# A two-layer streaming-encoder trunk on one core: two groups share their first halves of K at the start, and one more chunk is done in seven products at the end

## The chip, the cores and the metric

The kernel runs on one core of one Trainium2 chip. The metric is the device time of one execution in microseconds (us), as a median over runs. The engines are TensorE (PE in the profile, with its weight loads as PEld), VectorE (DVE), ScalarE (ACT), GpSimd (POOL) and SyncE (SP). SP and ACT issue the DMAs here, on a queue each; the rows of those issues stand under SPq and ACTq.

## The reference, cut to what matters

Two layers (DEPTH = 2) of 256 frames with 1024 channels in float32:

```python
for i in range(2):
    x = x + 0.5 * swiglu(rmsnorm(x, ffn1_norm[i]), w_gate, w_up, w_down)   # d_ff = 2816
    proj = rmsnorm(x, mix_norm[i]) @ w_in[i]
    ...                                       # self-attention (chunked, or differential), memory attention
    x = x + concat([o_s, o_m]) @ w_out[i]
    x = x + 0.5 * swiglu(rmsnorm(x, ffn2_norm[i]), w_gate, w_up, w_down)

def swiglu(h, w_gate, w_up, w_down):
    return (silu(h @ w_gate) * (h @ w_up)) @ w_down
```

The change touches the first half-step of layer 0 (its start) and the second half-step of layer 1 (the last work of the kernel).

## The kernel before, in words

**Products.** Every float32 operand is split into a high part `hi` (a cast to the type fp32r, by ACT at L338) and a remainder `lo` = operand - `hi` (by DVE at L356). A product of a 128x128 block of x with a 128x512 block of weights is three matmuls of 512 columns in `dense`: hi by xh (L511), lo by xh (L514), hi by xl (L517). So each block of weights costs one cast and one remainder before PE can use it, and PE does them all in the order in which they were recorded.

**Weights.** They come in chunks of four blocks into three buffers `raw` (`NRAW = 3`), all loads issued by SP (L294). In `ffn`, a gate-and-up chunk (g, c) holds 256 columns of `w_gate` and 256 of `w_up` of group g (of NG = 11), for the half c of K = 1024: four blocks k of 128 rows. Group g adds up in two PSUM banks `gu`, one for each half-tile of 128 frames (tb = 0, 1), over both chunks, (g, 0) and then (g, 1). The first chunk of the kernel is loaded in eight pieces of 128 KB (gate and up of each block), the second in four of 256 KB, later ones in two of 512 KB.

**x.** It stands in two tiles, `x0` and `x1` (x_85 and x_86 in the order), one for each tb. `prep_half(xt, tb, hf, ...)` takes one half hf of 512 channels: four transposes on PE (`xtp`, L525), y = transposed x by the gain (DVE, L557), xh (ACT cast, L560), xl (DVE, L562). Channel half hf is K half c of the first products. The squares of x for the norm are summed by ACT (`junk`, L574) and come in later, as a factor of the result. Four sums and differences of the y tiles (L780) with casts and remainders `xf` (L784, L787) follow for a pair of groups that is done with seven products.

**The start.** `start_gain` and `start` are threads with times written by hand. In between PE does some products of the identity (`warm`). The load of ACT's function table is asked for by `table_hint`.

**Down.** The down chunks c = 0 to 10 (256 rows of `w_down` each) take 8 products of 3 matmuls. A chunk in the table `SEVEN` takes 7: `seven_item` forms four sums of weight blocks (`wsum`, DVE), and `seven_forms` four sums of the hidden values (`sf`); results go to four more banks `m`, which `seven_sums` adds into x after the last such chunk. The first such chunk holds two pairs of hi and lo buffers; a later one (`guest`) puts part of its blocks into the room of xh and xl (`gxh`, `gxl`), of which there is one.

**What sets the order.** The program is recorded by threads in a small planner (`Flow`) with a clock of its own, estimated durations (`flow.act`, `flow.dve`) and arrival times for loads (`dma_free`, `LAT`); each engine then does its instructions in the recorded order. The last small loads (`late_loads`, among them the rows `grow` of gains) are issued by SP one behind each later chunk; PE transposes `grow` (`gps`, L231) 8 us of the planner's clock after the last.

**DMAs and semaphores.** Each DMA gets one of eight completion semaphores (DMAHW0 to DMAHW7 in the order below), one after the other in the order of the built program, whichever queue issues it. A DMA that gets a semaphore which an earlier one has used waits, where it is issued, for that one's landing.

Of the kernel before, what the change touches and what calls it, by code (L numbers as in the profile page):

```python
# [16 lines left out]
AF = mybir.ActivationFunctionType  # L17
# [3 lines left out]
P = 128  # L21
# [121 lines left out]
def kernel(  # L143
# [10 lines left out]
    nc = tc.nc  # L154
    PSUM = bass.MemoryType.PSUM
    NRAW, NHL, NT2 = 3, 4, 19
    flow = Flow()
# [19 lines left out]
    def bank(name, shape=(P, 4, P)):  # L177
        return banks.take(list(shape), F32, name)
# [3 lines left out]
    nc.scalar.dma_start(out=g1row, in_=ffn1_norm.rearrange("l (k p) -> (l k) p", p=P))  # L182
    xs = [const.tile([P, D], F32, name=f"x{tb}") for tb in range(2)]

    def load_x(tb, hf, queue=None):
        (queue or nc.sync).dma_start(out=xs[tb][:, hf * 512:(hf + 1) * 512],
                                     in_=x[0, tb * P:(tb + 1) * P, hf * 512:(hf + 1) * 512])

    load_x(0, 0)
    load_x(1, 0, nc.scalar)  # L190

    ident = const.tile([P, P], F32, name="ident")
    make_identity(nc, ident)
# [78 lines left out]
    raw_left = [NRAW]  # L272
    hl_left = [NHL]
    xt_room = [False]
    dma_free = [2.5]
    LAT = 1.5
    at = [0]

# [4 lines left out]
    def add_chunk(parts, uses=8, w=1):  # L283
        return Item([add_raw(parts)], uses, w)

    def loader():
        for i, c in enumerate(chunks):
            yield lambda: raw_left[0] > 0
            raw_left[0] -= 1
            c.raw = wraw.tile([P, 2048], F32, tag="raw", name=f"raw{i}")  # L290
            dma_free[0] = max(dma_free[0], flow.now)
            n = len(c.parts)
            for j, (dst, src) in enumerate(c.parts):
                nc.sync.dma_start(out=dst(c.raw), in_=src)  # L294
                dma_free[0] += 2.9 / n
                if i < 2 and j % 2:
                    for q in range((j - 1) * 4 // n, (j + 1) * 4 // n):
                        c.block[q] = dma_free[0] + LAT
                if i == 1 and j == 1:
                    load_x(1, 1)  # L300
                    dma_free[0] += 0.7
            c.arrive = dma_free[0] + LAT
            c.block = [t or c.arrive for t in c.block]
            if i == 0:
                load_x(0, 1)
                dma_free[0] += 0.7
            if i > 4 and late_done[0] < len(late_loads):
                dst, src = late_loads[late_done[0]]
                late_done[0] += 1
                nc.sync.dma_start(out=dst, in_=src)  # L310
                dma_free[0] += 0.3
# [56 lines left out]
    def cols4(w, c, c0, n, o, pieces=1):  # L368
        st = 4 // pieces
        return [((lambda raw, a=a: k4(raw)[:, a:a + st, o:o + n]),  # L370
                 w[c * 512 + a * P:c * 512 + (a + st) * P, c0:c0 + n].rearrange("(k p) n -> p k n", p=P))
                for a in range(0, 4, st)]
# [1 line left out]
    def rows2(w, r):  # L374
        return [(lambda raw: k2(raw), w[r * 256:(r + 1) * 256, :].rearrange("(k p) n -> p k n", p=P))]

    SEVEN = {(0, 1): (), (0, 2): (1, 4, 7), (1, 1): (1, 4, 7), (1, 2): (1, 4, 7)}
    PAIR = {(0, 1): 4, (0, 2): 3, (1, 1): 3, (1, 2): 3}

    def turned2(w, r):  # L380
        src = w[r * 256:(r + 1) * 256, :].rearrange("(k b i) n -> b i k n", k=2, b=4)
        return [((lambda raw, b=b: k2(raw)[b::4]), src[b]) for b in range(4)]
# [6 lines left out]
    def seven_item(it, guest):  # L389

        r = [it.own(q) for q in range(4)]
        t = lambda j: lambda: it.t[j]
        it.n, it.uses, it.takes, it.gives, it.guest = 1 if guest else 2, 7, 4, 4, guest
        it.sums = [(r[1], r[0]), (r[3], t(0)), (r[3], r[1]), (r[2], t(1))]
        it.units = [(r[0], 0, 1, None), (r[2], 1, 1, None), (r[3], 2, 1, None)] + [(t(j), 3 + j, 1, j) for j in range(4)]
# [46 lines left out]
    def plan_ffn(l, nm, wg, wu, wd):  # L442
        def parts(g, c):
            pieces = (4, 2)[len(chunks)] if len(chunks) < 2 else 1
            a = cols4(wg[l], c, g * 256, 256, 0, pieces)
            b = cols4(wu[l], c, g * 256, 256, 256, pieces)
            return [q for ab in zip(a, b) for q in ab]

        gu = {}
        pair = PAIR[l, nm]  # L450
        work = [(g, c) for g in range(NG) for c in range(2)]
        if pair is not None:
            rest = [w for w in work if w[0] not in (pair, pair + 1)]
            n = 2 * pair
            p = iter(rest[n:])
            work = rest[:n]
            loads = {}
            for x in ("11", "m1", "p", "12", "m5", "p", "22", "m7", "p", "m6", "p", "m3", "p", "p", "21", "m2", "p", "m4"):
                work.append(next(p) if x == "p" else x)
            work += list(p)  # L460
            blocks = {"11": (pair, 0), "12": (pair + 1, 0), "22": (pair + 1, 1), "21": (pair, 1)}
            raws = [Chunk(parts(*blocks[x])) for x in ("11", "12", "22", "21")]
            made, mk = pair_items(raws)
            which = dict(zip(("11", "12", "22", "21"), raws))
        for w in work:
            if w in ("11", "12", "22", "21"):
                chunks.append(which[w])
            elif isinstance(w, str):
                mk[w]()
            else:  # L470
                gu[w] = add_chunk(parts(*w), 8, 2)
        plan[l, nm, "gu"] = gu
        plan[l, nm, "work"] = [w for w in work if w not in ("11", "12", "22", "21")]
        if pair is not None:
            plan[l, nm, "pair"] = made
        dn = []
        for c in range(NG):
            dn.append(add_chunk(turned2(wd[l], c)))
            if c in SEVEN[l, nm]:
                seven_item(dn[-1], c != SEVEN[l, nm][0])  # L480
            elif c >= NG - 3:
                u = dn[-1].units
                u[1], u[2] = u[2], u[1]
        plan[l, nm, "dn"] = dn
# [133 lines left out]
    def ffn(l, nm, xt, gc_next):  # L618
        hts = [None] * NG
        htt = [None] * NG  # L620
        sv = SEVEN[l, nm]
        prog = [-1]
# [127 lines left out]
        def plain_chunk(g, c, tbs, ks=range(4)):  # L750
            if g not in open_:
                flow.until(banks.has(2))
                open_[g] = [bank(f"gu{tb}", (P, 512)) for tb in range(2)], [None, None]
                flow.spawn(evac(g, *open_[g]))
            ps, end = open_[g]
            for tb in tbs:
                for k in ks:
                    kk = 4 * c + k
                    t = dense(ps[tb], xt.h[tb][:, kk, :], xt.l[tb][:, kk, :], lambda: xt.t[tb][kk],
                              plan[l, nm, "gu"][g, c], k, kk == 0, kk == KT - 1)  # L760
                if c == 1 and 3 in ks:
                    end[tb] = t
# [85 lines left out]
        work = list(plan[l, nm, "work"])  # L848
        if (l, nm) != (0, 1):
            for tb in range(2):  # L850
                for c in range(2):
                    plain_chunk(0, c, (tb,))
        else:
            for c in range(2):
                for ks in ((0, 1), (2, 3)):
                    plain_chunk(0, c, range(2), ks)
        work = work[2:]
        for w in work:
            if isinstance(w, str):
                product(w)  # L860
# [47 lines left out]
    def table_hint(func):  # L908
        nc.scalar.activation(dummy, dummy, func)
        flow.act(1, 1.3)  # L910
# [710 lines left out]


    flow.spawn(loader(), idle=True)
    flow.spawn(split_hi(), idle=True)
    flow.spawn(split_lo(), idle=True)
# [3 lines left out]
    def start_gain():  # L1629
        tp = bank("gps0")  # L1630
        nc.tensor.transpose(out=tp[:, 0, :16], in_=g1row, identity=ident[:16, :16])
        yield flow.pe(T_TR)
        nc.vector.tensor_copy(gcol[:, 0:16], tp[:, 0, :16])
        banks.give()
        flow.dve(16)
        warm(2)
        yield 4.6
        warm(5)

    def start(tb, hf, t):  # L1640
        yield t
        yield from prep_half(xt, tb, hf, GC_FFN1, 3.0)

    def warm(n):
        for _ in range(n):
            nc.tensor.matmul(out=wb[:, 0, :], lhsT=ident, rhs=ident, start=True, stop=True)
# [1 line left out]
    wb = bank("warm")  # L1648
    banks.give()
    warm(4)  # L1650
    table_hint(AF.Silu)
    flow.now = 2.7
    flow.spawn(start_gain())
    for tb in range(2):
        for hf in range(2):
            flow.spawn(start(tb, hf, (3.4, 8.8, 5.6, 10.8)[2 * tb + hf]))
    flow.spawn(gain_columns())
    flow.spawn(rope_setup(), idle=True)
    flow.spawn(lambda_setup())
# [2 lines left out]
    for l in range(DEPTH):  # L1662
        xt = ffn(l, 1, xt, GC_MIX + l * KT)
        xt = mixer(l, xt, GC_FFN2 + l * KT)
        xt = ffn(l, 2, xt, None if l == DEPTH - 1 else GC_FFN1 + (l + 1) * KT)
# [53 lines left out]
```

## Time and profile before

| what | value |
|---|---|
| median of 3 runs | 954.87 us (954.74 to 955.77) |
| profiled execution | 955.69 us |
| its span (first to last instruction) | 953.9 us, so 1.8 us lie around it |
| granted TensorE clock | 1.0 |
| busy: PE, PEld, DVE, ACT, POOL | 945.6, 774.1, 820.0, 587.0, 109.1 us |
| HBM read and written | 188.99 MB, 14.16 MB: 213 GB/s over the span |

A busy share is an average over stages. Where PE has work without a gap, only its own work counts; where it waits, the row of the wait names what came last. In the rows of the timeline stand start, duration, engine, line, operation, tiles and, in brackets, how long the engine was idle and for what. In the rows by stretch stand length and busy time of each engine with the number of instructions, then granted clock, share of the DMA engines and GB/s. In the rows of the DMA view the last number is the median time from issue to landing.

### The profile page before, as it was taken

The numbers are of one execution on the slowest core, as the hardware profiler recorded it, in microseconds if no ns is written. First come the engines' busy times: TensorE is split into PE (matmuls) and PEld (weight loads), VectorE is DVE, ScalarE is ACT, GpSimd is POOL, SyncE is SP. The second block draws the span as 40 slices with busy tenths as digits, with TensorE's granted clock in tenths as the row PEclk, the third lists the DMA queues.
The fourth block names the chain that finished last, engine by engine and source line by source line (L and its number), as shares of the span: only waits on it lengthen the run. The fifth ranks groups of instructions, "written<-read, shape, count | busy, mean of one in ns | idle before, by whom it ended". The sixth has DMA issues, their size and how long they took to land.

```text
span 953.9 us, 13334 instructions
## 1 busy us (share of the span) xinstructions
PE 945.6 (99%) x4475; PEld 774.1 (81%) x4475; DVE 820.0 (86%) x1483; ACT 587.0 (62%) x1121; POOL 109.1 (11%) x160
## 2 busy tenths in 40 slices
PE   9999999999999999999999999999999999999998
PEld 7888888887777888888888888888787778888886
DVE  7898978888777899979889899796999888999884
ACT  6556566677676746647546656564676865665650
POOL 1000057621210100000000000000434200000000
PEclk9999999999999999999999999999999999999999
DMA  8987799486525387887746679775641367588751
GB/s 265 289 263 236 224 354 296 158 276 210 177 90 177 97 266 225 262 287 219 245 146 219 208 226 288 247 253 166 196 158 57 121 214 228 183 275 276 239 197 45
DMA packets 169887, 204.04 MB, mean 214 GB/s; under 512 B 10137, under 2 KB 145114, under 8 KB 169818
## 3 DMA queue, kind: packets, MB, share of 16 engines
q1 hardware_dynamic: 169498, 202.78, 66.0%
q8 instruction: 35, 0.57, 0.3%
q10 hardware_dynamic: 320, 0.40, 0.1%
q14 instruction: 34, 0.28, 0.1%
HBM read 188.99 MB, written 14.16 MB: 213 GB/s over the span
## 4 chain that ended last, share of the span: by engine, by line
PE 90%; DVE 6%; DMA 2%; ACT 1%; issue 1%; SPq 0%; ACTq 0%; DVEq 0%
PE gu L517 13%; PE gu L514 13%; PE gu L511 13%; PE acc L511 9%; PE acc L517 9%; PE acc L514 9%; PE pair_m L511 3%; PE pair_m L514 3%; PE pair_m L517 3%; PE pj L517 2%; PE pj L511 2%; PE pj L514 2%; DVE lo L356 2%; PE S L1360 1%; DMA x<-in_x_dram 1%; PE AV L1441 1%
## 5 line engine op out<-in xcount | busy, mean ns | idle before, releaser
L338 ACT CAST hi<-raw 128x512 fp32r<-128x512 f32 (+1 forms) x467 | 336.3, 770 | 172.6 <-DMA raw<-in_ffn_w_up_dram 45.6
L356 DVE TENSOR_TENSOR lo<-raw,hi 128x512 fp32r<-128x512 f32 (+1 forms) x467 | 391.9, 875 | 35.5 <-ACT hi L338 35.4
L514 PE MATMUL gu<-lo,xh 128*128 128x512 f32 x576 | 224.7, 390 | 0.5 <-DVE lo L356 0.5
L517 PE MATMUL gu<-hi,xl 128*128 128x512 f32 x576 | 224.5, 390 | 0.4 <-DVE xl L562 0.4
L511 PE MATMUL gu<-hi,xh 128*128 128x512 f32 x576 | 224.4, 390 | 0.0
L517 PEld LDWEIGHTS gu<-hi,xl 128*128 128x128 f32 x576 | 108.1, 188 | 23.9 <-DVE xl L562 1.7
L514 PEld LDWEIGHTS gu<-lo,xh 128*128 128x128 f32 x576 | 108.1, 188 | 23.5 <-DVE lo L356 1.4
L511 PEld LDWEIGHTS gu<-hi,xh 128*128 128x128 f32 x576 | 108.2, 188 | 22.3
L517 PE MATMUL acc<-hi,ht 128*128 128x512 f32 x280 | 109.5, 391 | 0.0
L511 PE MATMUL acc<-hi,ht 128*128 128x512 f32 x280 | 109.2, 390 | 0.0
L514 PE MATMUL acc<-lo,ht 128*128 128x512 f32 x280 | 109.1, 390 | 0.0
L338 ACT CAST hi<-wsum 128x512 fp32r<-128x512 f32 x82 | 47.7, 619 | 26.5 <-DVE wsum L350 26.5
L514 PE MATMUL pj<-lo,xh 128*128 128x512 f32 x160 | 64.0, 400 | 0.0
L517 PE MATMUL pj<-hi,xl 128*128 128x512 f32 x160 | 63.8, 399 | 0.0
L511 PE MATMUL pj<-hi,xh 128*128 128x512 f32 x160 | 63.8, 399 | 0.0
L514 PEld LDWEIGHTS acc<-lo,ht 128*128 128x128 f32 x280 | 52.6, 188 | 10.9
L517 PEld LDWEIGHTS acc<-hi,ht 128*128 128x128 f32 x280 | 52.6, 188 | 10.8
L511 PEld LDWEIGHTS acc<-hi,ht 128*128 128x128 f32 x280 | 52.6, 188 | 10.7
L532 POOL TENSOR_TENSOR xr<-v,nhalf 128x1 f32<-128x1 f32 x12 | 10.3, 861 | 435.1 <-DVE v L530 435.1
L356 DVE TENSOR_TENSOR lo<-wsum,hi 128x512 fp32r<-128x512 f32 x82 | 52.8, 680 | 0.0
L633 ACT ACTIVATE sil<-gu,xr 128x256 f32<-128x256 f32 x72 | 33.7, 468 | 29.8 <-PE gu L517 29.7
L532 POOL TENSOR_TENSOR hf<-v,nhalf 128x8 f32<-128x8 f32 (+1 forms) x20 | 31.4, 1570 | 87.3 <-DVE v L530 78.9
(232 smaller groups left out, 1429.5 us busy)
## 6 DMA issues: line engine op xcount, KB each, us to landing
raw<-in_ffn_w_down_dram SPq DMA_DIRECT2D x176, 256.0 KB, 4.5
raw<-in_ffn_w_gate_dram SPq DMA_DIRECT2D x82, 512.0 KB, 4.0
raw<-in_ffn_w_up_dram SPq DMA_DIRECT2D x82, 512.0 KB, 5.4
raw<-in_w_in_dram SPq DMA_DIRECT2D x32, 512.0 KB, 4.4
hd<-hb SPq DMA_DIRECT2D x44, 256.0 KB, 4.6
hr<-hd SPq DMA_DIRECT2D x44, 256.0 KB, 4.6
raw<-in_w_out_dram SPq DMA_DIRECT2D x8, 1024.0 KB, 5.1
raw<-in_w_mem_kv_dram SPq DMA_DIRECT2D x4, 1024.0 KB, 5.3
```

What stands on the lines that cost most here:

```text
L338: nc.scalar.copy(out=it.part(0, q, w), in_=src())
L356: nc.vector.tensor_sub(it.part(1, q, w), src(), it.part(0, q, w).bitcast(F32))
L511: nc.tensor.matmul(out=ps, lhsT=xh, rhs=wh, start=start, stop=False)
L514: nc.tensor.matmul(out=ps, lhsT=xh, rhs=wl, start=False, stop=False)
L517: nc.tensor.matmul(out=ps, lhsT=xl, rhs=wh, start=False, stop=stop)
L532: nc.gpsimd.tensor_tensor(out=dst, in0=v[:, :n], in1=nhalf[:, :n], op=ALU.pow)
L633: nc.scalar.activation(sil, ps[tb][:, 0:256], AF.Silu, scale=xt.r[tb])
L1360: nc.tensor.matmul(out=ss[e][:, pr, :nk], lhsT=q[rows, pr, :], rhs=k[rows, pr, :], start=i == 0, stop=i == len(passes) - 1)
L1441: nc.tensor.matmul(out=av[64 * e:64 * e + 64, pr, :], lhsT=vsrc(kb, pr, e), rhs=pts[e][:, pr, kb, :], start=(kb == 0), stop=(kb == nb - 1))
```

## The change

At the start: x's first half-tile is loaded in two quarters, one on each queue; x1's first half goes behind the first weight pieces on SP; both second halves go behind both first chunks. Three pieces of the first chunk move to ACT's queue (the up piece of block 0, gate and up of block 3). The table load stands behind ACT's first issues. The plan of chunks becomes (0, 0), (1, 0), (0, 1), (1, 1), and so on: groups 0 and 1 both take their first halves of K before either takes its second. The planner's arrival times and the hand-written times change with it, and there are 4 warm products for 7 ahead of the first weights. At the end: chunks 1, 3, 5, 7 of the last down phase are in `SEVEN` instead of 1, 4, 7.

```diff
-    def load_x(tb, hf, queue=None):
-        (queue or nc.sync).dma_start(out=xs[tb][:, hf * 512:(hf + 1) * 512],
-                                     in_=x[0, tb * P:(tb + 1) * P, hf * 512:(hf + 1) * 512])
-
-    load_x(0, 0)
-    load_x(1, 0, nc.scalar)
+    def load_x(tb, hf, q=0, n=2, queue=None):
+        sl = slice(hf * 512 + q * 256, hf * 512 + (q + n) * 256)
+        (queue or nc.sync).dma_start(out=xs[tb][:, sl], in_=x[0, tb * P:(tb + 1) * P, sl])
+
+    load_x(0, 0, 0, 1)
+    load_x(0, 0, 1, 1, nc.scalar)
...
-    dma_free = [2.5]
+    dma_free = [2.95]
...
             n = len(c.parts)
+            lat = LAT if i > 1 else 0.6
             for j, (dst, src) in enumerate(c.parts):
-                nc.sync.dma_start(out=dst(c.raw), in_=src)
-                dma_free[0] += 2.9 / n
+                (nc.scalar if i == 0 and j in (1, 6, 7) else nc.sync).dma_start(out=dst(c.raw), in_=src)
+                dma_free[0] += 3.0 / n
                 if i < 2 and j % 2:
                     for q in range((j - 1) * 4 // n, (j + 1) * 4 // n):
-                        c.block[q] = dma_free[0] + LAT
-                if i == 1 and j == 1:
-                    load_x(1, 1)
-                    dma_free[0] += 0.7
-            c.arrive = dma_free[0] + LAT
+                        c.block[q] = dma_free[0] + lat
+                if i == 0 and j == 1:
+                    table_hint(AF.Silu)
+                    load_x(1, 0)
+                    dma_free[0] += 0.75
+            c.arrive = dma_free[0] + lat
             c.block = [t or c.arrive for t in c.block]
-            if i == 0:
-                load_x(0, 1)
-                dma_free[0] += 0.7
+            if i == 1:
+                for tb in range(2):
+                    load_x(tb, 1)
+                    dma_free[0] += 0.75
...
-    SEVEN = {(0, 1): (), (0, 2): (1, 4, 7), (1, 1): (1, 4, 7), (1, 2): (1, 4, 7)}
+    SEVEN = {(0, 1): (), (0, 2): (1, 4, 7), (1, 1): (1, 4, 7), (1, 2): (1, 3, 5, 7)}
...
         work = [(g, c) for g in range(NG) for c in range(2)]
+        if (l, nm) == (0, 1):
+            work[:4] = [(g, c) for c in range(2) for g in range(2)]
...
+            work = work[2:]
         else:
-            for c in range(2):
-                for ks in ((0, 1), (2, 3)):
-                    plain_chunk(0, c, range(2), ks)
-        work = work[2:]
+            for ks in ((0, 1), (2, 3)):
+                plain_chunk(0, 0, range(2), ks)
+            work = work[1:]
...
-        warm(2)
-        yield 4.6
-        warm(5)
+        yield 5.2
+        warm(4)
...
-    table_hint(AF.Silu)
...
-            flow.spawn(start(tb, hf, (3.4, 8.8, 5.6, 10.8)[2 * tb + hf]))
+            flow.spawn(start(tb, hf, (3.4, 12.0, 4.6, 13.0)[2 * tb + hf]))
```

What this makes of the order. In the rows, raw_111 is the first chunk; the second is raw_121 before and raw_122 now; hi_0 with a number is a chunk's cast, and xh_130 before is xh_132 now (tb = 0), xh_131 is xh_133 (tb = 1). In brackets stand the semaphores that an instruction waits for.

ACT's first instructions before:

```order
L182 DMA g1row<-in_ffn_norm_dram 16x128
L186 DMA x_86<-in_x_dram 128x512
L909 ACT_TABLE_LOAD
L909 ACTIVATE dummy<-dummy 128x1 [waits Pool_49]
L338 CAST hi_0_168<-raw_111 128x512 [waits DMAHW4_49,DMAHW3_49]
L560 CAST xh_130<-y 128x512 [waits DVE_49]
```

and now:

```order
L182 DMA g1row<-in_ffn_norm_dram 16x128
L187 DMA x_85<-in_x_dram 128x256
L295 DMA raw_111<-in_ffn_w_up_dram 128x256
L914 ACT_TABLE_LOAD
L914 ACTIVATE dummy<-dummy 128x1 [waits Pool_49]
L295 DMA raw_111<-in_ffn_w_gate_dram 128x256 [waits DMAHW1_49]
L295 DMA raw_111<-in_ffn_w_up_dram 128x256 [waits DMAHW2_49]
L341 CAST hi_0_162<-raw_111 128x512 [waits DMAHW4_49,DMAHW3_49]
L565 CAST xh_132<-y 128x512 [waits DVE_49]
```

Two issues with a semaphore to wait for stand ahead of ACT's first cast, where none stood. Which landings they are is told by SP's issues from the sixth on, each of which waits for the semaphore that it then takes:

```order
L295 DMA raw_111<-in_ffn_w_gate_dram 128x256 [waits DMAHW0_49]
L295 DMA raw_111<-in_ffn_w_up_dram 128x256 [waits DMAHW1_49]
L295 DMA raw_122<-in_ffn_w_gate_dram 128x2x256 [waits DMAHW2_49]
L295 DMA raw_122<-in_ffn_w_up_dram 128x2x256 [waits DMAHW3_49]
L295 DMA raw_122<-in_ffn_w_gate_dram 128x2x256 [waits DMAHW4_49]
L295 DMA raw_122<-in_ffn_w_up_dram 128x2x256 [waits DMAHW5_49]
L187 DMA x_85<-in_x_dram 128x512 [waits DMAHW6_49]
L187 DMA x_86<-in_x_dram 128x512 [waits DMAHW7_49]
L295 DMA raw_129<-in_ffn_w_gate_dram 128x4x256 [waits DMAHW0_49]
L295 DMA raw_129<-in_ffn_w_up_dram 128x4x256 [waits DMAHW3_49]
```

Between the last two, numbers 1 and 2 are missing: ACT's two issues have them, for their third use. Their second use is the up piece of block 2 (raw_111, number 1) and the second chunk's first gate piece (raw_122, number 2), so these landings are what ACT's issues wait for.

DVE's order in the opening before, from its first op on raw:

```order
L356 TENSOR_TENSOR lo_0_169<-raw_111,hi_0_168 128x512 [waits DMAHW4_49,DMAHW3_49,Activation_49]
L562 TENSOR_TENSOR xl_132<-y,xh_130 128x512 [waits Activation_49]
L557 TENSOR_TENSOR y<-xtp,gcol 128x512 [waits PE_49]
L356 TENSOR_TENSOR lo_0_169<-raw_111,hi_0_168 128x512 [waits DMAHW6_49,DMAHW5_49,Activation_49]
L356 TENSOR_TENSOR lo_0_169<-raw_111,hi_0_168 128x512 [waits DMAHW7_49,DMAHW0_49,Activation_49]
L356 TENSOR_TENSOR lo_0_169<-raw_111,hi_0_168 128x512 [waits DMAHW2_49,DMAHW1_49,Activation_49]
L562 TENSOR_TENSOR xl_133<-y,xh_131 128x512 [waits Activation_49]
L557 TENSOR_TENSOR y<-xtp,gcol 128x512 [waits PE_49]
```

and now, its first two ops on raw and then the stretch up to the third chunk (raw_129, the second half of K of group 0):

```order
L359 TENSOR_TENSOR lo_0_163<-raw_111,hi_0_162 128x512 [waits DMAHW4_49,DMAHW3_49,Activation_49]
L562 TENSOR_TENSOR y<-xtp,gcol 128x512 [waits PE_49]
L567 TENSOR_TENSOR xl_134<-y,xh_132 128x512 [waits Activation_49]
L359 TENSOR_TENSOR lo_0_163<-raw_111,hi_0_162 128x512 [waits DMAHW7_49,DMAHW6_49,Activation_49]
...
L359 TENSOR_TENSOR lo_0_200<-raw_122,hi_0_199 128x512 [waits Activation_49]
L562 TENSOR_TENSOR y<-xtp,gcol 128x512 [waits PE_49] x2
L567 TENSOR_TENSOR xl_134<-y,xh_132 128x512 [waits Activation_49]
L567 TENSOR_TENSOR xl_135<-y,xh_133 128x512 [waits Activation_49]
L785 TENSOR_TENSOR y<-y 128x512 [waits DVE_49] x4
L792 TENSOR_TENSOR xf<-y,xf 128x512 [waits Activation_49]
L359 TENSOR_TENSOR lo_0_261<-raw_129,hi_0_260 128x1024 [waits DMAHW3_49,DMAHW0_49]
```

The y of tb = 1 moved ahead of the first xl, and the second halves' y and xl moved behind all eight remainders of the first two chunks; the third chunk's first remainder now has four of the sums and one xf ahead of it. On PE, whose order follows the table of chunks, the first 24 matmuls take raw_111 for both tb, the next 24 raw_122, and the transposes of x's second halves stand behind the 23rd and the 26th.

## The prediction

> **What bounds the kernel now.** I read the page's engine shares first, then the list of waits of TensorE (PE), then the opening row by row.
>
> ```profile
> span 953.9 us, 13334 instructions
> PE 945.6 (99%) x4475; PEld 774.1 (81%) x4475; DVE 820.0 (86%) x1483; ACT 587.0 (62%) x1121; POOL 109.1 (11%) x160
> ```
>
> PE is busy for 99% of the span. Its waits are few; the three that the opening holds are these (us in total, times, longest):
>
> ```profile
> PE gu L514 <- DVE lo L356: 0.5, 1, 0.5
> PE gu L517 <- DVE xl L562: 0.4, 1, 0.4
> PE xtp L525 <- DMA x<-in_x_dram: 0.3, 1, 0.3
> ```
>
> So there are two ways to shorten this kernel: fewer matmuls, or less idle PE at its two ends. The other side holds too: what makes PE idle is paid in full, since nothing later has slack to give it back. The stretches of the opening, with busy us of PE, PEld, DVE, ACT, POOL, and PE's rows around its idle time:
>
> ```profile
> 7.00:12.60 5.60, 4.64 (x22) 2.41 (x21) 4.82 (x8) 3.92 (x10) 0.00 (x0) 1.00 0.96 313
> 12.60:22.60 10.00, 10.00 (x47) 8.27 (x46) 9.66 (x18) 8.74 (x18) 1.86 (x2) 1.00 0.94 303
> ...
> 4.59 1.06 PE L525 MATMUL xtp<-ident,x 128*128 128x128 f32 x4
> ...
> 7.13 0.48 PE L511 MATMUL gu<-hi,xh 128*128 128x512 f32 x1
> ...
> 9.01 0.50 PE L514 MATMUL gu<-lo,xh 128*128 128x512 f32 x1 [0.48 <-DVE lo L356]
> ...
> 10.06 0.66 PE L525 MATMUL xtp<-ident,x 128*128 128x128 f32 x4 [0.31 <-DMA x<-in_x_dram]
> ...
> 12.20 0.66 PE L525 MATMUL xtp<-ident,x 128*128 128x128 f32 x4
> ...
> 12.61 0.48 PE L514 MATMUL gu<-lo,xh 128*128 128x512 f32 x1
> 12.93 0.40 PE L517 MATMUL gu<-hi,xl 128*128 128x512 f32 x1
> ...
> 13.16 0.40 PE L511 MATMUL gu<-hi,xh 128*128 128x512 f32 x1
> ```
>
> The first real matmul starts at 7.13 and the eleventh at 12.61. From there they follow each other every 0.227 us (12.93 to 13.16), 44 of them in the stretch 12.60:22.60. Ten at that pace and two sets of transposes, some 0.45 each (10.06 and 12.20), need 2.27 + 0.9 = 3.2 of those 5.5 us: PE loses 2.3 us there, which is all that an opening can win. In the same second stretch VectorE (DVE) is busy for 9.66 of 10 us: it is as full as PE.
>
> **The opening: who issues, and what stands behind it.** These rows are the price list.
>
> ```profile
> 1.18 0.44 ACTq L186 DMA_DIRECT2D x<-in_x_dram  x1
> 1.65 1.28 ACT L909 ACT_TABLE_LOAD   x1 [1.65 <-PEq L1698]
> 4.02 0.48 SPq L294 DMA_DIRECT2D raw<-in_ffn_w_gate_dram  x1
> 5.09 0.33 SPq L294 DMA_DIRECT2D raw<-in_ffn_w_up_dram  x1
> 5.51 0.62 ACT L338 CAST hi<-raw 128x512 fp32r<-128x512 f32 x1 [2.36 <-DMA raw<-in_ffn_w_up_dram]
> 6.30 0.68 DVE L356 TENSOR_TENSOR lo<-raw,hi 128x512 fp32r<-128x512 f32 x1
> 6.94 1.14 ACT L338 CAST hi<-raw 128x512 fp32r<-128x512 f32 x2
> 7.07 0.69 DVE L562 TENSOR_TENSOR xl<-y,xh 128x512 fp32r<-128x512 f32 x1
> 7.67 0.68 DVE L557 TENSOR_TENSOR y<-xtp,gcol 128x512 f32<-128x512 f32 x1
> 8.28 1.28 DVE L356 TENSOR_TENSOR lo<-raw,hi 128x512 fp32r<-128x512 f32 x2
> 10.43 0.63 ACT L574 ACTIVATE junk<-x 128x512 bf16<-128x512 f32 x1
> 10.96 0.19 ACT L574 ACTIVATION_READ_ACCUMULATOR junk<-x 128x1 f32 x1
> 16.76 2.15 DVE L780 TENSOR_TENSOR y<-y 128x512 f32<-128x512 f32 x3
> 18.82 0.15 DVE L583 TENSOR_TENSOR sst<-xss 128x1 f32<-128x1 f32 x1
> 19.68 1.22 DVE L356 TENSOR_TENSOR lo<-raw,hi 128x1024 fp32r<-128x1024 f32 x1
> ...
> x<-in_x_dram ACTq DMA_DIRECT2D x1, 256.0 KB, 3.9
> ...
> g1row<-in_ffn_norm_dram ACTq DMA_DIRECT2D x1, 8.0 KB, 2.5
> ...
> raw<-in_ffn_w_up_dram SPq DMA_DIRECT2D x2, 256.0 KB, 5.7
> ```
>
> The order of issue in the section on the change shows that the kernel has eight completion semaphores for its DMAs, taken in turn, and that a DMA whose semaphore is still in use is held until the earlier one has landed. What that costs can be seen here: SP issues one weight piece at 4.02 and the next only at 5.09 instead of 4.5. That one takes the semaphore of the x load issued on ACT at 1.18, which lands 3.9 later, at 5.08.
>
> In the changed kernel two such DMAs stand on ACT's queue, ahead of ACT's first cast. The gate piece of block 3 takes semaphore 1 after the up piece of block 2; the up piece of block 3 takes semaphore 2 after the second group's first gate piece (raw_122, 256 KB, SP's eighth DMA). ACT does its instructions in order (table load at 1.65, right behind the issue that ends at 1.62), so its first cast waits until SP's eighth DMA has landed. No row shows ACT held by a DMA, so I bound it. SP's eighth issue stood at 4.02; it now waits for x's quarter on ACT's queue (issued at 1.18, landing 2.5 to 3.9 later, 3.7 to 5.1): 4.0 to 5.1. A landing took 2.5 (8 KB) to 5.7 (256 KB behind others). So ACT is free between 6.5 and 10.8; I take 4.1 + 3.9 = 8.0, by the 256 KB load that was issued at the same early stage. With 0.44 for the last issue the first cast starts at 8.45 instead of 5.51.
>
> [...]
>
> DVE is next. Its casts' remainders run every 0.61 us (7.07, 7.67, 8.28); the first follows the first cast by 0.79 (5.51 to 6.30): 9.24. The new order puts y of the second half-tile ahead of xl: lo 9.24, y 9.85, xl 10.46, lo 11.07. In the old trace a matmul started 0.73 after its remainder (8.28 to 9.01), so the third matmul starts at 11.2 and the fifth at 11.8 (9.01 before). Then PE has first-half work of both groups: 44 more matmuls and two sets of transposes, 10.0 + 0.9, until 22.7, when it wants the first remainder of raw2 (second half of K).
>
> That is far down DVE's queue. After 11.07: xl and two lo (12.9), then the second chunk's four lo. Those follow ACT's casts, 0.52 apart (6.94, two in 1.14) with two squares of 0.72 (10.43 to 11.15) between: their casts start at 13.15, 13.67, 14.9 and 15.4, the last remainder at 16.3. Then y and xl of both second halves, whose transposes stand in PE behind the 23rd and 26th matmul (16.6 and 17.8): xl at 18.4 and 19.2. Four sums of 0.72 (2.15 for three) from 19.8, one remainder of 0.61, and lo of 1.22: done at 24.5. PE waits 1.8. The second lo of raw2 comes after four ops of 0.15 (0.5 in all), 0.61 and 1.22: 26.8; six matmuls take PE to 25.9, and it waits 0.9 more. So the 56th matmul starts at 26.8; before it started at 12.61 + 45 x 0.227 = 22.8. **Opening: +4.0 us** (2.5 with ACT free at 6.5, 6.8 with 10.8). This is where the old kernel had 0.6 to spare: lo of raw2 ended at 20.9, its matmul stood at 12.61 + 39 x 0.227 = 21.5.
>
> Costed at nothing: three warm matmuls less, and the table load behind the first issues (PE and ACT wait there anyway; without the hold the load would run from 2.05 to 3.3, before weights land); x in quarters of 1 KB rows (hidden by the hold on ACT); x's second halves as SP's 12th and 13th DMA, issued near 6.5 and landed by 12.2 even at 5.7, wanted at 16.1. POOL issues none of this.
>
> **Later.** DVE's lag delays its freeing of the three raw buffers, and so every SP load. One small load is close behind:
>
> ```profile
> 78.29 0.36 SPq L310 DMA_DIRECT2D grow<-in_b_subln_dram  x1
> ...
> 83.79 0.27 PE L231 MATMUL gps<-ident,grow 55*128 55x55 f32 x1
> ...
> raw<-in_ffn_w_up_dram SPq DMA_DIRECT2D x82, 512.0 KB, 5.4
> ```
>
> PE transposes it 5.5 us after its issue, and the load just ahead of it lands 5.4 after its own in the median. What DVE lags more than PE shows here: nothing up to 1.5 us (PE has waited 2.7 for DVE by then, so both lag alike); I take 0.5, since DVE is 22.57 of 24 us busy at 60 to 84 and can't catch up.
>
> **The end.** One more chunk takes seven products for eight: 3 matmuls x 0.227 = 0.68 us less. It adds four sums, three casts and three remainders of 512 columns, and small forms: DVE 7 x 0.61 + about 1.5 = 5.8 us, ACT 3 x 0.52 + 0.5 = 2.1.
>
> ```profile
> 60.00:84.00 24.00, 24.00 (x108) 19.57 (x106) 22.57 (x33) 15.12 (x22) 0.00 (x0) 1.00 0.72 230
> ...
> 890.00:910.00 20.00, 20.00 (x90) 16.57 (x89) 19.20 (x34) 14.63 (x29) 0.00 (x0) 1.00 0.73 229
> 910.00:930.00 20.00, 20.00 (x90) 16.58 (x89) 16.99 (x33) 11.68 (x24) 0.00 (x0) 1.00 0.54 179
> 930.00:950.00 20.00, 20.00 (x90) 16.41 (x88) 9.69 (x15) 1.89 (x4) 0.00 (x0) 1.00 0.11 40
> ```
>
> At 910 to 950 DVE has 3.0 + 10.3 us idle, ACT 26: covered. The new chunk 5 reuses room that chunk 3 gives back; chunk 4 with 24 matmuls (5.4 us) lies between, and the first pair needs 1.4. If that cover went, at most one such pair, 1.4 us, would be seen; the gain stands at 0.68 (from +0.7 to -0.7 in time).
>
> **Sum.** +4.0 + 0.5 - 0.7 = +3.8 us. The profiled execution took 955.69 (1.8 around its span) and would take 959.5, span 957.7; it lies 0.8 over the median of 954.87. Against the median: **958.7**.
>
> **Rivals.** (a) The hold on ACT costs nothing, because the eighth DMA lands by 5.1 or ACT isn't held. Then the first cast stands near 5.5, DVE's queue 3.0 us earlier and the 56th matmul at 23.8, 1.0 later than before, or no later where DVE then waits less for ACT: with the end 954.2 to 955.2. For it: no row shows such a hold on ACT; against: SP's. (b) Faster: PE works without a gap from 7.1, since it has 48 matmuls that need only first halves. All 2.3 us are won, with the end 951.9. It decides if lo of raw2 is ready by 21; against it DVE's 9.66 of 10. (c) PE, idle before its first matmul, loses its clock and runs the first 15 matmuls at half speed: +3.4. In the old trace four early transposes took 1.06, later ones 0.66. These matmuls lie ahead of the 1.8 + 0.9 that PE waits for DVE, so only 0.7 would show, 959.4. [...] (d) An early landing (6.5) and no wait at 83.8: 2.5 - 0.7, 956.7, not to be told from no change.
>
> **Chances.** This kernel's runs differ by 0.1%, so 0.2% (1.9 us) is about what can be told from no change. Forecast and (c) together 0.80 (0.72 and 0.08), 956.8 to 962.5; (a) 0.11 and (d) 0.03, no change; (b) 0.06. Range: from 955.5, part of (a), to 962.0, a landing at 10.0.
>
> **What would show it.** ACT's first cast at 8 or later, right behind its own issue of an up piece; a wait of PE for lo of raw2 of 1 to 3 us around 24; the 56th matmul near 26.8; at the end the same gap-free PE with three matmuls less, the last one 0.7 us nearer to the group work before it. A first cast before 6, or no wait of PE around 21 to 27, proves me wrong.

## The result and the profile after

The changed kernel took 969.53 us in the median of five runs (967.12 to 971.0); the kernel before, run beside it, 955.1 (954.74 to 956.53). The ratio is 1.0147, 95% interval 1.0131 to 1.0163: slower by 14 us. The profiled execution took 971.0, span 969.2, which is 15.3 more than the span before.

The page's first lines and the waits of PE (us in total, times, longest) of the changed kernel:

```profile
span 969.2 us, 13330 instructions
PE 951.4 (98%) x4466; PEld 777.1 (80%) x4466; DVE 826.9 (85%) x1496; ACT 589.3 (61%) x1126; POOL 109.2 (11%) x160
```
```profile
PE gps L231 <- DMA hd<-hb: 4.7, 1, 4.7
PE gu L516 <- ACT xh L565: 2.8, 1, 2.8
PE gu L519 <- DVE lo L359: 2.6, 3, 1.6
```

The two lower waits lie in the opening. The first is new and stands at gps, PE's transposition of the small rows in `grow`: 83.79 before, 97.03 now. (The row names hd, a DMA issued 0.4 us behind `grow`'s last row; gps reads `ident` and `grow` alone, and releasers are inferred.) Nothing in the shares shows it; the list of waits does at once.

The opening, on ACT (start, duration, instruction, idle time ahead and what ended it), and the two waits of PE for the third chunk:

```profile
6.94 0.34 ACTq L295 DMA_DIRECT2D raw<-in_ffn_w_gate_dram  x1
9.38 0.33 ACTq L295 DMA_DIRECT2D raw<-in_ffn_w_up_dram  x1
9.82 0.62 ACT L341 CAST hi<-raw 128x512 fp32r<-128x512 f32 x1 [6.19 <-DMA raw<-in_ffn_w_gate_dram]
...
15.36 0.62 ACT L341 CAST hi<-raw 128x512 fp32r<-128x512 f32 x1 [2.42 <-DMA raw<-in_ffn_w_up_dram]
```
```profile
28.31 0.50 PE L519 MATMUL gu<-lo,xh 128*128 128x512 f32 x1 [1.57 <-DVE lo L359]
...
30.56 0.50 PE L519 MATMUL gu<-lo,xh 128*128 128x512 f32 x1 [0.59 <-DVE lo L359]
```

ACT issues the two pieces of block 3 at 6.94 and 9.38 and casts for the first time at 9.82, right behind its own issue. The last up piece, which left at 9.38, is waited for until 15.36. The 56th matmul starts at 30.56; before, it started at 22.95.

The later loss, on SP and on PE, and its window (us, then busy time of PE, PEld, DVE, ACT, POOL with counts, granted clock of TensorE as a share of full speed, DMA share, GB/s). In the rows hd is the store of a group's hidden values to HBM, and hr the load that brings them back in another layout; a pair chunk is one of the chunks, in eight loads, of the two groups that are done with seven products:

```profile
61.83 0.34 SPq L655 DMA_DIRECT2D hd<-hb  x1
66.53 0.37 SPq L661 DMA_DIRECT2D hr<-hd  x1
67.01 0.44 SPq L295 DMA_DIRECT2D raw<-in_ffn_w_gate_dram  x1
...
92.28 0.37 SPq L313 DMA_DIRECT2D grow<-in_b_subln_dram  x1
```
```profile
97.03 0.32 PE L231 MATMUL gps<-ident,grow 55*128 55x55 f32 x1 [4.73 <-DMA hd<-hb]
97.29 0.79 PE L519 MATMUL gu<-lo,xh 128*128 128x512 f32 x1
97.88 0.63 PE L522 MATMUL gu<-hi,xl 128*128 128x512 f32 x1
98.31 0.63 PE L516 MATMUL gu<-hi,xh 128*128 128x512 f32 x1
...
103.00 0.44 PE L522 MATMUL gu<-hi,xl 128*128 128x512 f32 x1
```
```profile
91.00:104.00 13.00, 7.93 (x22) 5.93 (x23) 10.82 (x17) 3.89 (x6) 0.00 (x0) 0.74 0.84 265
```

SP issues hd at 61.83 and then nothing for 4.4 us: next in its queue stands hr, which reads what hd wrote, and behind hr the eight loads of a pair chunk. Before, a load stood there (61.93). `grow`'s last small row leaves 14 us later than before (92.28 for 78.29), PE only 8.5 later. PE then waits 4.73 at gps, and the 14 matmuls behind it follow each other every 0.43 us, not every 0.23: the granted clock is 0.74 in that window, half from 96.25 to 103.07 and full in the rest. Below, the clock "closes" when it goes to half.

So the 15.3 are: 8.5 by which PE arrives late at gps (97.03 - 4.73 - 83.79), of which the opening has 7.6 (30.56 for 22.95) and small waits ahead of gps the rest; 4.7 waited there; 2.7 in the slow matmuls; and -0.7 at the end.

### The profile page after: what moved, and what is told of

It reads as the page before. It is cut to its first block, busy times and chain, and to the rows that moved or that the text cites. A ratio compares the mean times of both kernels' runs of the same rounds, so it can differ in the third digit from the quotient of the medians.

```text
span 969.2 us, 13330 instructions
## 1 busy us (share of the span) xinstructions
PE 951.4 (98%) x4466; PEld 777.1 (80%) x4466; DVE 826.9 (85%) x1496; ACT 589.3 (61%) x1126; POOL 109.2 (11%) x160
## 4 chain that ended last, share of the span: by engine, by line
PE 79%; DVE 9%; DMA 7%; ACT 2%; issue 1%; SPq 1%; POOL 0%; ACTq 0%; DVEq 0%; POOLq 0%
PE gu L522 11%; PE gu L519 11%; PE gu L516 11%; PE acc L516 8%; PE acc L522 8%; PE acc L519 8%; DVE lo L359 4%; DMA raw<-in_ffn_w_up_dram 3%; PE pair_m L519 2%; PE pair_m L516 2%; PE pair_m L522 2%; PE pj L522 2%; PE pj L519 2%; PE pj L516 2%; PE S L1365 1%
## 5 line engine op out<-in xcount | busy, mean ns | idle before, releaser
L519 PE MATMUL gu<-lo,xh 128*128 128x512 f32 x576 | 227.2, 394 | 2.6 <-DVE lo L359 2.6
L522 PE MATMUL acc<-hi,ht 128*128 128x512 f32 x272 | 106.4, 391 | 0.0
L516 PE MATMUL acc<-hi,ht 128*128 128x512 f32 x272 | 106.1, 390 | 0.0
L519 PE MATMUL acc<-lo,ht 128*128 128x512 f32 x272 | 106.0, 390 | 0.0
L522 PEld LDWEIGHTS acc<-hi,ht 128*128 128x128 f32 x272 | 51.1, 188 | 10.5
L516 PEld LDWEIGHTS acc<-hi,ht 128*128 128x128 f32 x272 | 51.1, 188 | 10.3
```

The costliest lines, as they stand in the source:

```text
L516: nc.tensor.matmul(out=ps, lhsT=xh, rhs=wh, start=start, stop=False)
L519: nc.tensor.matmul(out=ps, lhsT=xh, rhs=wl, start=False, stop=False)
L522: nc.tensor.matmul(out=ps, lhsT=xl, rhs=wh, start=False, stop=stop)
```

## The experiments

"PE's lag" is the start of gps less its own wait, against 83.79 in the kernel before; or, where gps was moved, the start of the same matmul of PE's order in both traces.

**Take the hold off ACT.**

```
-(nc.scalar if i == 0 and j in (1, 6, 7) else nc.sync).dma_start(...)
+(nc.scalar if i == 0 and j == 1 else nc.sync).dma_start(...)
```

> Block 3's two pieces go out on SP again; ACT's queue keeps one early piece; all else is the changed kernel. Theory A (the hold on ACT makes the opening's loss, and the lag of DVE that it leaves makes PE wait at gps): ACT's first cast at 5 to 6, PE's start of matmul 56 at 23 to 24 (30.6 with the hold, 22.8 before), no wait of several us at gps, no closed clock there; 955 to 956.5, against 955.1 before and 969.5 changed. Theory B (the later loss comes from SP's new order, hr ahead of the next raw loads, whatever the opening does): the opening gets its 7 us back, the wait of some 4.7 and the closed clock of some 2.7 at gps stay; 961 to 963. Theory C (the opening's loss lies in the chunk order, by DVE's queue, not in the hold): the first cast is early but PE waits for lo as before; 965 or more.

964.23 us (962.15 to 966.7), ratio 1.0093 [1.0079, 1.0107]. The median lies 1.2 over theory B's range, short of C's; the trace is what B says, with A false for the second loss and C for the opening:

```profile
5.82 0.62 ACT L341 CAST hi<-raw 128x512 fp32r<-128x512 f32 x1 [2.19 <-DMA raw<-in_ffn_w_up_dram]
...
89.24 0.24 PE L231 MATMUL gps<-ident,grow 55*128 55x55 f32 x1 [3.86 <-DMA raw<-in_ffn_w_up_dram]
```

The first cast stands at 5.82 and PE's lag falls from 8.5 to 1.6 (89.24 - 3.86 - 83.79). These 1.6 are in the trace's list as two waits for lo, 2.2 in all. The wait at gps stays, 3.86, though the opening is nearly on time.

**Move gps instead, with and without the hold.**

```
-        yield flow.now + 8.0
+        yield flow.now + 25.0
```

> The changed kernel with PE's transposition of grow (gps) 78 rows later in PE's order, some 18 us; the opening as it was. Theory A: PE's wait of 4.7 and the closed clock behind it (2.7) go and nothing takes their place; drift against before stays near 8 from 30 us to the end; 969.5 - 7.4 = 962. Rival: PE merely waits elsewhere, for lo of the next raw buffers, which are as late as grow was; 965 to 969.5.

> The two edits together: block 3's pieces on SP and gps later. Theory A: as without the later gps, 954.5 to 956.5, since no wait is left there. Theory B: 7 us less than with the hold removed alone, near 955. Theory C: 957 or more.

late_gps: 968.93 us, ratio 1.0138 [1.0122, 1.0153], not 962. both: 963.74, ratio 1.0083 [1.007, 1.0096], not 955. My theory missed both times. The rows of late_gps, then of both:

```profile
190.17 1.12 PE L530 MATMUL xtp<-ident,x 128*128 128x128 f32 x4 [3.69 <-DVE x L611]
190.93 0.78 PE L516 MATMUL acc<-hi,ht 128*128 128x512 f32 x1
191.51 0.63 PE L519 MATMUL acc<-lo,ht 128*128 128x512 f32 x1
```
```profile
182.09 0.66 PE L530 MATMUL xtp<-ident,x 128*128 128x128 f32 x4 [2.33 <-DVE x L611]
```

gps no longer waits, and PE waits at the end of the first feed-forward half, for DVE's update of x, with a closed clock behind it. gps is only where the loads' lag shows first. What has to be mended is the lag.

**Keep PE busy ahead of its first gu matmul.** The edit is `warm(18)` for `warm(4)` in `start_gain`.

> The changed kernel with 14 more warm matmuls ahead of PE's first gu matmul, so that PE works from 8.2 to about 11 where it was idle. Theory A (the closed clock of the opening is covered by PE's waits for lo of raw2, as the prediction had it): matmuls 0.227 apart from the start, PE waits that much longer for lo, at most 0.7 us won: 968.5 to 970. Rival (the closed clock is paid in full, 15 matmuls of 0.2 us more): 966 to 967.

967.7 us (964.17 to 972.16), ratio 1.0125 [1.0093, 1.0157], too wide to tell 966.5 from 969. The trace tells: eleven pairs of matmuls between 13.0 and 17.7 stood 0.43 apart in the changed kernel, none does here (PE does 52 matmuls in its 10.17 busy us from 11 to 22, for 37 in 10.80), and PE waits 3.4 for lo in place of 2.6. PE's lag at gps is 8.3 for 8.5. The slow clock of the opening costs 0.2 there: it is covered, as the prediction's rival (c) had it.

**The new order of chunks alone, in the kernel before.**

```
+        if (l, nm) == (0, 1):
+            work[:4] = [(g, c) for c in range(2) for g in range(2)]
...
-            for c in range(2):
-                for ks in ((0, 1), (2, 3)):
-                    plain_chunk(0, c, range(2), ks)
-        work = work[2:]
+            for ks in ((0, 1), (2, 3)):
+                plain_chunk(0, 0, range(2), ks)
+            work = work[1:]
```

> The kernel before with the new order of the first chunks alone; its DMAs (sizes, queues, x in halves), start times, warm matmuls and three seven-product chunks at the end stay as they were. Theory B (the order of chunks makes the planner put each hr ahead of the next pair chunk's loads on SP; SP is held, the weights come late, PE waits at gps): opening within 1.5 of before, a wait of PE at gps of 3 to 5 us with a closed clock of 1 to 3 behind it; 960 to 963 against 955.1. Rival (the order is harmless; the second queue, the quarters of x and the start times bring the loss that stays without the hold): 954 to 956.

962.96 us (962.18 to 965.87), ratio 1.0076 [1.0063, 1.009]: theory B.

```profile
53.43 0.34 SPq L652 DMA_DIRECT2D hd<-hb  x1
59.03 0.37 SPq L658 DMA_DIRECT2D hr<-hd  x1
59.91 0.35 SPq L294 DMA_DIRECT2D raw<-in_ffn_w_gate_dram  x1
...
88.39 0.32 PE L231 MATMUL gps<-ident,grow 55*128 55x55 f32 x1 [4.19 <-DMA raw<-in_ffn_w_up_dram]
```

The order costs little in the opening (lag 0.4), and 6.5 us at gps (4.2 waited, 2.3 in slow matmuls): SP is held for 5.3 us between hd and hr, and the pair chunk that was issued at 52.48 before leaves at 59.91.

**hr off SP's queue.** The one line moves 11 transfers from SP to POOL and leaves the order of TensorE's, DVE's and ACT's instructions as it was (the same in both traces). It also gives hr semaphores of its own (DMASW0 to DMASW7 in the built program), so SP's other DMAs come round to their eight a little later. That this is not what held SP is told by an hr of the changed kernel whose hd has a landing in the trace: hd, issued at 73.05, lands 6.3 later, and hr leaves SP at 79.33.

```
-            nc.sync.dma_start(out=hr, in_=hd...)
+            (nc.gpsimd if (l, nm) == (0, 1) else nc.sync).dma_start(out=hr, in_=hd...)
```

> The kernel before with the new order of the first chunks, and the hr transfers of the first feed-forward half issued from POOL's queue; nothing else is moved on any engine. Theory B (SP stands behind an hr that waits for hd's landing, and the weights behind it come late): the loads after each hr are issued as soon as their buffer is free, the wait of 4.2 at gps and the closed clock (2.3) go; 955.5 to 957.5, against 962.96 with hr on SP. Rival D (the raw buffers are freed late by ACT and DVE whatever SP does): 961 to 963.

> The changed kernel with the hr transfers of the first feed-forward half on POOL's queue alone. Theory B: the opening keeps its 7.6 to 8.3, the wait at gps and the closed clock (7.7 in all) go or fall under 1.5, the end keeps its -0.7: 962 to 964, against 969.5. Rival E (the 14 us by which the loads lag after the opening's hold are there without hr's hold too): 967 or more.

order_hr_pool (order_only with this line): 958.21 us (956.07 to 962.67), ratio 1.0025 [1.001, 1.004]. after_hr_pool (the changed kernel with it): 963.27 (961.93 to 965.06), ratio 1.0074 [1.0061, 1.0087]. The rows of order_hr_pool, then gps of after_hr_pool:

```profile
53.30 0.34 SPq L652 DMA_DIRECT2D hd<-hb  x1
55.19 0.34 SPq L294 DMA_DIRECT2D raw<-in_ffn_w_gate_dram  x1
...
58.41 0.75 POOL L658 DMA_DIRECT2D hr<-hd  x1 [8.80 <-DVE h L638]
...
84.50 0.26 PE L231 MATMUL gps<-ident,grow 55*128 55x55 f32 x1 [0.23 <-DMA grow<-in_b_subln_dram]
```
```profile
91.26 0.26 PE L231 MATMUL gps<-ident,grow 55*128 55x55 f32 x1
```

With hr on POOL the same loads leave at 55.19 for 59.91, gps waits 0.23 for 4.19, and no matmul behind it is slow. In the changed kernel the wait is gone as well, and what is left is the opening: 91.26 - 83.79 = 7.5. So in these two kernels the second loss is SP's place behind an hr that waits, shown by taking hr off SP and nothing else in any engine's order. The median of order_hr_pool lies 0.7 over its range and 2 us over its profiled 956.12; its runs spread over 6.6 us, and no trace here shows a slower one, so what makes those slower stays open.

The issues that the line takes off SP are little in themselves: eleven of 0.37 us, spread over some 100 us. The transfers ran no faster from POOL (in the median, hr lands 4.9 after its issue from POOL in order_hr_pool, and 4.6 to 5.5 after one from SP there, in order_only, in the changed kernel and in the one before). What the line saved is the wait that stands ahead of the issue, 5.3 us at the one hr above (53.77 to 59.03).

**Put hr later on SP.** In place of another queue, a longer delay in the planner, on top of no_hold.

```
-            yield flow.now + 2.0
+            yield flow.now + (2.5 if (l, nm) == (0, 1) and g < 4 else 2.0)
```

> The changed kernel with block 3's pieces on SP and, in the first feed-forward half, the planner's delay between hd and hr longer by 0.5 us for groups 0 to 3, which moves three hr on SP behind the eight loads of a pair chunk that they stood ahead of. Theory B: the third pair chunk (raw_609) is issued near 54 and not at 59.6, the wait at gps and its closed clock (3.9 and 1.4) go, and the drift stays near 1.6 to the end; 956 to 959, against 964.2 without the longer delay. Rival D (DVE frees the raw buffers that late anyway, and hr's place costs nothing): 963 to 965.

961.39 us (959.75 to 963.98), ratio 1.0056 [1.0041, 1.0072]: between the two. The rows of SP, ACT and DVE:

```profile
51.09 2.47 SPq L661 DMA_DIRECT2D hr<-hd  x2
...
59.17 0.34 SPq L295 DMA_DIRECT2D raw<-in_ffn_w_gate_dram  x1
...
55.39 0.62 ACT L670 CAST ht<-hr 128x512 fp32r<-128x512 f32 x1 [3.52 <-DMA hr<-hd]
...
56.66 2.49 DVE L353 TENSOR_TENSOR wsum<-raw,raw 128x512 f32<-128x512 f32 x4
```

The pair chunk again leaves at 59.17. SP isn't held there now; the buffer is, until DVE has read it (56.66 + 2.49 = 59.15), and DVE stood behind ht, ACT's cast of an hr that came late (at 56.05 DVE had waited 2.34 for it). The stall went from SP to ACT and DVE, and gps waits 2.7.

**Which of the two pieces holds ACT.** The changed kernel with hr on POOL and only the gate piece of block 3 on ACT (`j in (1, 6)`).

> The changed kernel with the hr transfers of the first feed-forward half on POOL's queue and only the last up piece back on SP; block 3's gate piece stays on ACT's queue. Theory F (two holds: each costs until another DMA has landed, and the last up piece, issued after the second hold, lands 5.9 later still): ACT's first cast at 7 to 7.5, no second wait of ACT for that up piece, the 76th matmul 2.5 to 4.5 behind before (7.5 with both holds, 1.6 with none); 958 to 960.5 against 963.3. Rival G (the first hold and DVE's queue make it): 962 or more.

961.93 us (960.2 to 964.21), ratio 1.0066 [1.0052, 1.0079].

```profile
7.11 0.33 ACTq L295 DMA_DIRECT2D raw<-in_ffn_w_gate_dram  x1
7.55 0.62 ACT L341 CAST hi<-raw 128x512 fp32r<-128x512 f32 x1 [3.92 <-DMA raw<-in_ffn_w_up_dram]
...
89.60 0.24 PE L231 MATMUL gps<-ident,grow 55*128 55x55 f32 x1 [1.89 <-DMA raw<-in_ffn_w_up_dram]
```

PE's lag is 3.9 (89.60 - 1.89 - 83.79), with none of the two 1.6 (no_hold), with both 7.5 (after_hr_pool): the first hold costs 2.3, the last up piece 3.6, its hold and its late landing together. Theory F for the opening. The time is over its range, because gps waits 1.9 here though hr is on POOL. Some of the loads' lag thus has another source; I take it to be DVE's order (next), but that pair of edits wasn't tried with one hold.

**DVE's order behind the opening.** On top of no_hold, the four sums and remainders of the pair's x forms later in the plan.

```
             yield lambda: len(xt.y) == 4 and g4.left >= 4
+            if (l, nm) == (0, 1):
+                yield flow.now + 6.0
```

> The changed kernel with block 3's pieces on SP and, in the first feed-forward half, the four sums and four remainders of the pair's x forms 6 us later in the plan, so that DVE makes the remainder of raw2 ahead of them. Theory: PE's waits for lo (2.2 us in all without this edit) fall under 0.7, and the opening ends some 1 us ahead of before in place of 1.6 behind; the wait at gps stays, since hr stands ahead of the pair chunk on SP as before: 960 to 962.5. Rival (PE then waits for another late remainder): 963 to 965.

956.84 us (956.06 to 960.2), ratio 1.0012 [1.0001, 1.0023], 3 us better than the best I expected. The edit did more than it was meant to: the planner now puts a chunk between hd (51.98) and hr (54.42) on SP, and the pair chunk behind leaves at 55.98, in no_hold at 59.55. So the shorter wait at gps has two sources here, and no run separates them. In the opening, DVE makes lo of raw2 at 18.29 in place of 21.04 in no_hold, the list of PE's waits has none for lo, and from 22 to 32 PE is busy all the time (here, and in no_hold):

```profile
22.00:32.00 10.00, 10.00 (x46) 8.29 (x45) 9.52 (x18) 6.87 (x11) 0.93 (x1) 1.00 0.73 237
```
```profile
22.00:32.00 10.00, 9.10 (x39) 7.21 (x40) 8.93 (x15) 7.27 (x10) 1.19 (x2) 1.00 0.64 206
```

PE is 0.6 to 0.9 ahead of before until gps, where it waits 1.6. So the new order's opening can win up to 0.9, if DVE doesn't put the sums of a product that comes much later ahead of remainders that PE wants next.

**The end alone**, in the kernel before.

```
-(1, 2): (1, 4, 7)}
+(1, 2): (1, 3, 5, 7)}
```

> The kernel before with chunks 1, 3, 5 and 7 in seven products in its last feed-forward half. Prediction's term: three matmuls of 0.227 less and no new wait, -0.68: the profile's last matmul 0.6 to 0.7 earlier against the same matmul before, the time 0.7 less in the median (0.07%, at the edge of what can be told). Rival (the added sums on DVE are seen at the end): no gain, or up to 0.7 more.

955.41 us, ratio 0.9993 [0.9985, 1.0002]: by time not to be told. By the trace it is -0.68: a matmul ahead of the last groups, and PE's last one, in the kernel before and in this one.

```profile
872.31 0.39 PE L517 MATMUL gu<-hi,xl 128*128 128x512 f32 x1
...
949.83 0.39 PE L517 MATMUL acc<-hi,ht 128*128 128x512 f32 x1
```
```profile
873.16 0.39 PE L517 MATMUL gu<-hi,xl 128*128 128x512 f32 x1
...
950.00 0.39 PE L517 MATMUL acc<-hi,ht 128*128 128x512 f32 x1
```

0.85 behind at the one (from small waits in the middle), 0.17 at the other.

**Mended versions.** best1 has the edits of no_hold, forms_late and late_gps; best2 also hr on POOL; old_order is the kernel before with hr on POOL, the later gps and the fourth seven-product chunk.

> The changed kernel with block 3's pieces on SP, the x forms' sums 6 us later in the plan, and gps some 80 rows later in PE's order. Theory: opening -0.9, no wait at gps (1.6 and some closed clock in the kernel without the later gps), end -0.7: 953.5 to 955.5, against 955.1 to 956.1 before. Rival (the lag of the loads, 3.5 us there, shows at the end of the first half instead, near 180 us, as it did without the later sums, where it cost 4.1): 956 to 959.

> The kernel of the entry ahead with the hr transfers of the first feed-forward half on POOL's queue as well. Theory B: loads ahead of their need throughout, no wait of PE after the opening: 953.5 to 955. Rival (POOL's queue brings its own delay to hr, and ht comes late): 956 or more.

> The kernel before (its chunk order, its DMAs at the start) with the hr transfers of the first feed-forward half on POOL's queue, gps 80 rows later and the fourth seven-product chunk at the end. Theory H (the new order's opening wins up to 0.9 by itself): 0.3 to 0.9 above the mended version of the changed kernel (954.86), 955 to 956. Rival (the order wins nothing; what the mended version wins is the end's -0.7): 954.3 to 955.

best1: 955.14 us, ratio 0.9986 [0.9977, 0.9994]. best2: 954.86, ratio 0.9984 [0.9976, 0.9993], with no wait of PE over 0.6 us behind its first. Both are faster than the kernel before beside them (956.51) by 0.14 to 0.16%; that is under the 0.2% that I had called the bound, but the intervals leave 1 out. old_order: 956.13, ratio 1.0002 [0.9993, 1.0011]; that is just over theory H's range. Its trace gains 0.7 at the end and stands 0.9 behind ahead of it, from small waits. That points to the new order as the source of best2's gain, but the intervals touch and the runs were not side by side, so it isn't shown.

The runs beside each other (PE's lag and its wait at gps from the trace; ratio of the time to the kernel before):

| kernel | PE's lag at gps, us | wait at gps, us | ratio, 95% interval |
|---|---|---|---|
| changed | 8.5 | 4.7 | 1.0147 [1.0131, 1.0163] |
| no_hold | 1.6 | 3.9 | 1.0093 [1.0079, 1.0107] |
| one_hold (hr on POOL) | 3.9 | 1.9 | 1.0066 [1.0052, 1.0079] |
| after_hr_pool | 7.5 | 0 | 1.0074 [1.0061, 1.0087] |
| order_only | 0.4 | 4.2 | 1.0076 [1.0063, 1.009] |
| order_hr_pool | 0.5 | 0.2 | 1.0025 [1.001, 1.004] |
| hr_late | 2.5 | 2.7 | 1.0056 [1.0041, 1.0072] |
| forms_late | -0.9 | 1.6 | 1.0012 [1.0001, 1.0023] |
| best2 | -0.2 | 0 | 0.9984 [0.9976, 0.9993] |

## Why the prediction was wrong

It said slower, by 3.8; it is 14.4. The way was right, and so was the hold on ACT; the later term had the wrong mechanism. By its own terms:

- **ACT held by two DMA issues**: right. The first cast stands right behind ACT's own issue of an up piece, and without the hold at 5.82.
- **U, the landing of SP's eighth DMA**: 9.4, not 8.0; issued at 4.47 (4.1 assumed), landed 4.9 later (3.9 assumed). Inside the bounds given, and 1.4 of the miss.
- **The last up piece's own landing**: left out. I let ACT's casts run back to back from 8.45. But that piece leaves only behind the hold and lands 5.9 later; its cast waits 2.42, to 15.36. I had the fourth remainder done at 12.9; it was done at 16.69. These 3.8 (1.4 and 2.4) arrive whole at the 56th matmul, 30.56 for 26.8. one_hold shows what this piece costs with its hold: 3.6.
- **Opening +4.0**: 7.6 (the sum put the 56th matmul before at 22.8; its row says 22.95). PE's two waits for lo of raw2 are there, 1.57 and 0.59 for 1.8 and 0.9, at 28 for 24.
- **Rival (c), the clock**: right in what it forecast, the first matmuls at half speed (14 from 11.01 to 17.74, for 15 assumed), and wrong in why. It has PE's idle stretch close the clock. That stretch was 2.78, but it closed nothing: the warm products ahead of it were already 0.213 apart, up to 7.81, so the clock had not opened yet (its first record in the trace is the opening at 17.74; the column of the granted clock says 1.00 ahead of it, and only the pace tells). Before, they go from 0.213 to 0.112 at 5.88. Why it opens later now (fewer warm products, waits for x's quarters) no run separates. (c) let 0.7 of it show; 0.2 did, since PE waits for DVE behind it (warm_more).
- **Rivals (a), (b) and (d)**: the first cast at 9.82, the waits for lo and the landing at 9.4 speak against them.
- **Later +0.5**: the step that failed most; 7.4 (4.7 and 2.7). I priced what DVE's lag does to the loads, and took PE's lag off it. What delays them is another thing: the new order of chunks makes the planner put each hr on SP ahead of the next pair chunk's loads. I read SP's order through the opening and not beyond it, though the change shifts everything that the planner places later. It happens without any hold in the opening (order_only, 6.5 us) and goes when hr leaves SP's queue (after_hr_pool). The small row's slack of 5.5 us from issue to use was seen, and that no other slack stands behind it; not that the clock would close behind PE's wait and cost half as much again (2.7 on 4.7).
- **The end -0.68**: right (-0.68 in the changed kernel's trace and in tail_only's).

## What to carry to other kernels

In these kernels a DMA that waited held what stood behind it on its issuing engine: on ACT the casts (the first at 9.82 for 5.82), on SP the next loads (59.91 for 55.19); and where the held thing was itself a load, its own landing came on top (5.9 for the last up piece). When a change goes through a planner, read the order of every queue to the end of the stage and not only at the place of the edit, above all where a transfer that waits for another has changed sides with loads that don't. A wait taken away at the place where it showed (late_gps) was waited elsewhere, since its source stood (4.73 at gps, then 3.69 at the end of the first half).

## What the runs showed of the hardware that I had not expected

TensorE's clock closed behind idle stretches to which my forecast gave no cost. Behind waits of 2.33, 2.70, 3.86, 4.19 and 4.73 us (both, hr_late, no_hold, order_only, the changed kernel) came 6 to 13 matmuls 0.43 apart. Behind waits of 2.2, 3.69 and 4.3 (late_gps in its opening, late_gps again, warm_more) the granted clock was 0.84 from 11 to 22, 0.94 from 140 to 200 and 0.74 from 91 to 104. Around waits of 1.6 (the changed kernel in its opening, no_hold, both, forms_late) it was 1.00. Waits of 1.89 to 1.92 went both ways: no slow matmul behind three (one_hold twice, warm_more), some 3.4 us of slow ones behind two (after_hr_pool, late_gps). In no_hold, order_only and the changed kernel the closing cost 1.6, 2.3 and 2.7 us on top of its wait.

The granted clock shows more. In the changed kernel's trace it opens at 17.74, closes at 96.25 and opens again at 103.07: 78.51 and 6.83 us apart, which are 23 and 2 times 3.41. In after_hr_pool PE was idle for 1.89 of the 3.41 us from 24.41, and the clock was half in the 3.42 behind them; in warm_more PE was idle for 1.76 of the 3.41 from 26.44, and the clock was 1.00 from 25 to 32. The longest wait for lo was 1.9 in both (the rows of after_hr_pool, then of warm_more; PE's busy time comes first behind the length):

```profile
24.41:27.82 3.41, 1.52 (x7) 0.98 (x6) 3.33 (x7) 3.38 (x9) 0.00 (x0) 1.00 0.06 18
27.82:31.24 3.42, 3.42 (x9) 2.58 (x9) 3.40 (x5) 3.42 (x5) 1.18 (x2) 0.50 0.09 16
```
```profile
26.44:29.85 3.41, 1.65 (x6) 1.05 (x6) 3.34 (x9) 3.41 (x6) 1.18 (x2) 1.00 0.00 0
```

These three traces agree with a clock that changes at steps of 3.41 us. How long PE has to be idle within one for it to close they don't tell beyond these figures.

Half speed lasted 6.83 us in the changed kernel (96.25 to 103.07) and 3.42 in after_hr_pool. In `both` the slow stretch began well behind the wait: PE works again from 182.09, and the matmuls are 0.23 apart up to 183.51 and 0.43 from 183.88 to 186.87:

```profile
183.28 0.39 PE L516 MATMUL acc<-hi,ht 128*128 128x512 f32 x1
183.51 0.57 PE L519 MATMUL acc<-lo,ht 128*128 128x512 f32 x1
183.88 0.63 PE L522 MATMUL acc<-hi,ht 128*128 128x512 f32 x1
...
186.87 0.44 PE L516 MATMUL acc<-hi,ht 128*128 128x512 f32 x1
```
